# RWKV recurrence: output products of four chunks in one group, grams over 64 rows, wider zero products over the whole recurrence, and three more weight tiles for the experts

## The chip, the cores and the metric

One Trainium2 chip, one of its cores. The metric is the time of the program on the device in microseconds; lower is better. TensorE is called PE below, VectorE DVE, ScalarE ACT, GpSimd POOL, SyncE SP.

## The reference, cut to what matters

A backbone of two layers over 512 latent tokens and 256 context tokens of width 1024, all in float32. Layer 0 mixes attention with a convolution; layer 1 mixes RWKV-7 time mixing with a neighbourhood attention. Each layer ends in a mixture of 16 experts. The change lies in layer 1.

```python
def wkv7_step(S, inp):
    r, w, k, v, a, b = inp
    sa = jnp.einsum('bhvk,bhk->bhv', S, a)
    S = S * w[:, :, None, :] + sa[..., None] * b[:, :, None, :] + v[..., None] * k[:, :, None, :]
    return S, jnp.einsum('bhvk,bhk->bhv', S, r)
...
    y = head_group_norm(y_lat[0] + y_lat[1], gn_g, gn_b) * lat[6]
...
    gate, idx = lax.top_k(jnp.swapaxes(aff, 1, 2), cap)
    xs = jax.vmap(lambda hb, ib: hb[ib])(h, idx)
    hid = jax.nn.silu(jnp.einsum('becd,edf->becf', xs, w1)) * jnp.einsum('becd,edf->becf', xs, w3)
    ys = jnp.einsum('becf,efd->becd', hid, w2) * gate[..., None].astype(h.dtype)
```

The recurrence runs over the context and then the latent tokens, forwards and backwards, for 8 heads of 64 channels. Outputs of both directions are summed; only those of latent tokens are used, since layer 1 is the last.

## The kernel before, in words

The recurrence is computed in chunks of 64 tokens: 4 of context and 8 of latents. Two heads share the 128 partitions. Four pairs of heads times two directions are eight chains, n = 0 to 7; even n run forwards, odd n backwards, and n // 2 is the pair.

`rw_prep` (L1719 on) loads the decays, keys and queries of a chain, scales them and builds the grams G: 12 chunks x 2 heads of products `BK` by `RA` (L1763), four chunks to a group, each head to a PSUM bank of its own. `BK` holds zeros in the 64 rows that belong to the other head, and both operands are taken with all 128 rows. `rw_prep2` transposes `BK` (L1787). `rw_inverse` (L1922, L1930, L1945, L1959) inverts a triangular matrix for every chunk.

`rw_chain` (L1791 on) is the serial part, 12 steps a chain. A step multiplies the gram by the values (L1802) and the state by the queries (L1805), copies the sum out (X1, on ACT, L1807), multiplies it by the inverse (L1810), copies that into `UV` (L1812), and forms the next state `Z` from `pz` (L1817, then DVE L1821; POOL L1826 scales a copy). From step 4 on, the chunk is a latent one, and its output is accumulated in a bank `py`, which takes both directions of a pair of heads: per head a product `UV` by `G` (128 rows, 64 columns, L1836) and one `Z` by `RA` (64 rows, 64 columns, L1837). The bank is opened at step 4 of the forward chain by a product of zeros; at the end of the backward chain a term is added (L1842) and the sum copied to `yT`. There is one such bank.

`rw_run` advances everything in rounds n = -2 to 8 of 18 turns: in each turn the chain two or three times, the inverse of the chain two rounds ahead, the preparation of the one three rounds ahead, and the neighbourhood attention (`na_att`, L1426 to L1469). After each advance of the chain comes a zero product (`warm`, L1856): 128 rows and columns of zeros in bfloat16 by 224 columns, added to the open bank, as long as there is one. Rounds 6 and 7 also run `tail`: normalisation of finished heads and the output projection (`proj`, L545).

What is written is not the order that runs. A scheduler lays out each engine's queue ahead of time by its own model of the durations; a priority of 1000 is given to the chain. A queue is then executed in its fixed order.

The weights go through a ring of tiles of 1 MB, loaded by SP in a fixed sequence (`Ring.fill`, L150). A pool of tiles serves the phases that it is opened for. For the experts of layer 1 (phase 4) there are 9 tiles, opened at the end of the recurrence, and 8, opened in `layer1` when the projection's weights are done. The experts follow: `mix_tile` normalises, computes affinities and chooses tokens (`topk`, `choose`), `gather` fetches the rows of the first two experts (L684), and `experts` multiplies (w1 and w3 in L749, w2 in L815). Memory is cut from two arenas, "main" and "side". `open_x` reserves the residual X (4 x 1024 words) and `xT0` in one pool, which is held until the end of the experts.

Of the kernel before, what the change touches and what calls it, by code (L numbers as in the profile page):

```python
# [189 lines left out]
class Kern:  # L190
# [312 lines left out]
    def open_x(self, n=NT):  # L503

        self.right = ExitStack()
        xres = self.right.enter_context(self.arena.pool(1, True, ("m",)))
        self.X = [xres.tile([128, D], FT, name=f"X{t}") for t in range(n)]
        self.xT0 = xres.tile([128, 8, 128], FT, name="xT0")

    def open_ring(self, i):  # L510
        self.mring = ExitStack()
# [177 lines left out]
    def experts(self, i, ep, g2, cg2, with_ctx):  # L689
# [187 lines left out]
        if with_ctx:  # L877
            cT[0] = self.cT0
        more = ExitStack()
        with self.tc.manual_schedule(engines={mybir.EngineType.PE}):  # L880
            for p in range(8):
                H(p, 0)
                if p == i == 0:
                    more.enter_context(self.ring.open(self.arena, MOE_RING[1], (1,)))
                if p + 1 < 8:
                    prep_x(p + 1, 4)
                    prep_c(p + 1, 4)
                if p:
                    W2(p - 1, 1)
                H(p, 1)  # L890
                W2(p, 0)
            W2(7, 1)
# [342 lines left out]
    def layer1(self):  # L1235
        nc, tc, I = self.nc, self.tc, self.I
        with ExitStack() as ph:
# [36 lines left out]
            with ExitStack() as post:  # L1274
                self.rw_run(rw, post, yT, naT)
                self.open_ring(1)
                self.banks(NA_BANKS)
                for _ in self.rw_out(self.op, yT, 3):
                    pass
                todo = []  # L1280
                for t in range(4):
                    now = self.mix_tile(t, [yT, naT], (2, 3))
                    for f in now[:2]:
                        f()
                    if t == 3:

                        self.mix_done()
                        self.oring.close()
                        cs.close()
                        ph.enter_context(self.ring.open(self.arena, 8, (4,)))  # L1290
                    for f in todo:
                        f()
                    todo = now[2:]
                for f in todo:
                    f()
            self.moe(1, False)
        self.right.close()

# [296 lines left out]
    def rw_run(self, es, post, yT, naT):  # L1595
        nc, S, sets = self.nc, self.S, self.sets
        with ExitStack() as ae:
# [3 lines left out]
            py = {}  # L1601
            att = self.na_att(ap, naT)
            due = 0.0
            self.warmp = None
            emp = iter(())
            for n in range(-2, 9):
                chain = self.rw_chain(S[n], py, n // 2, yT[:, n // 2]) if 0 <= n < 8 else emp
# [11 lines left out]
                for i in range(18):  # L1619
                    if n >= 6 and i % 3 == 2:  # L1620
                        next(tail, None)
                    for x in range(2 + (i == 17)):
                        self.prio(chain, 1000)
                        self.warm(224)
                    self.prio(inv, 1000 if n < 0 else 0)
                    if i >= 3:
                        self.prio(prep2, 1000 if n < 0 else 0)
                    if i >= 6:
                        self.prio(prep, 1000 if n < 0 else 0)
                    due += ATT[min(n + 2, 3)][i]  # L1630
                    while due >= 1:
                        due -= 1
                        next(att, None)
# [81 lines left out]
    def rw_prep(self, hp, d, S):  # L1715
# [41 lines left out]
        for g in range(3):  # L1757
            ps = [self.bank("A") for h in range(2)]
            for a in range(4):
                c = 4 * g + a  # L1760
                i0 = c if g == 0 else IR(c)
                for h in range(2):
                    nc.tensor.matmul(ps[h][:, 128 * a:128 * a + 128], BK[:, c, 2 * h:2 * h + 2].rearrange("p a t -> p (a t)"),  # L1763
                                     RA[:, i0:i0 + 2].rearrange("p a t -> p (a t)"), start=True, stop=True)
            for h in range(2):
                p = ps[h]
                if g == 0:
# [24 lines left out]
    def rw_chain(self, S, pys, hp, y):  # L1792
# [1 line left out]
        nc, st = self.nc, self.st  # L1794
        d, RA, G, BKn, dec, UV, Q = (S[x] for x in ("d", "RA", "G", "BKn", "dec", "UV", "Q"))
        order = ORDER[d]
        Z = None
        p = self.bank(f"c{d}")
        px, pu, pz = p[:, 0:64], p[:, 64:128], p[:, 128:192]
        for i, c in enumerate(order):  # L1800
            for h in range(2):
                nc.tensor.matmul(px[HB[h]], G[HQ[h], h, IA(c)], UV[HQ[h], c, h], start=True, stop=(i == 0))  # L1802
            if i:
                for h in range(2):
                    nc.tensor.matmul(px[HB[h]], RA[HQ[h], IA(c)], Z[HQ[h]], start=False, stop=True)  # L1805
            X1 = st.tile([128, 64], FT, name=f"X1{d}")
            nc.scalar.activation(X1, px, AF.Copy)  # L1807
            yield
# [6 lines left out]
            if i < 11:  # L1815
                for h in range(2):
                    nc.tensor.matmul(pz[HQ[h]], BKn[:, c, h], UV[:, c, h], start=True, stop=True)  # L1817
                Zn = st.tile([128, 64], FT, name=f"Z{d}", bufs=4)
                de = dec[:, order[i + 1]:order[i + 1] + 1]
                if i:  # L1820
                    nc.vector.scalar_tensor_tensor(Zn, pz, de, Zd, op0=OP.mult, op1=OP.add)  # L1821
# [3 lines left out]
                    Zd = st.tile([128, 64], FT, name=f"Zd{d}", bufs=1)  # L1825
                    nc.gpsimd.tensor_scalar(Zd, Zn, dec[:, order[i + 2]:order[i + 2] + 1], None, op0=OP.mult)  # L1826
            if i >= 4:
                if i == 4 and d == 0:
                    pys[hp] = self.bank("y")
                    nc.tensor.matmul(pys[hp], self.zero[:, 0:128], self.zero, start=True, stop=False)  # L1830
                    self.warmp = pys[hp]
                py = pys[hp]
                for h in range(2):
                    q = HQ[h]
                    o = py[q, 64 * (c - 4):64 * (c - 4) + 64]
                    nc.tensor.matmul(o, UV[:, c, h], G[:, h, IR(c)], start=False, stop=False)  # L1836
                    nc.tensor.matmul(o, Z[q], RA[q, IR(c)], start=False, stop=False)  # L1837
            Z = Zn
            yield
        if d == 1:  # L1840
            self.warmp = None
            nc.tensor.matmul(py, self.ident, y, start=False, stop=True)  # L1842
            nc.scalar.activation(y, py, AF.Copy)

    def prio(self, g, o):

# [257 lines left out]
```

## Time and profile before

| | us |
|---|---|
| median of 3 runs | 2452.12 |
| lowest and highest | 2444.69, 2467.73 |
| the profiled execution | 2454.27 |
| its span, first to last instruction | 2452.5 |
| recurrence of layer 1, in the profile | 1417 to 1890 |
| experts of layer 1, from their first full stretch of loads | 1967 to 2452.5 |

A busy share is the time in which an engine has an instruction in hand. PE's instructions overlap, so a row's duration is longer than the distance to the next start. A float32 product is recorded as two instructions (two passes), except a transpose; a bfloat16 one as one. In the rows, 64*64 is the part of the array that is used (rows by columns), 64x64 the shape of what is written.

### The profile page before, as it was taken

What the parts mean: (1) busy time and instruction counts of PE and PEld (TensorE: products, weight loads), DVE (VectorE), ACT (ScalarE), POOL (GpSimd) and SP (SyncE); (2) the same over time, 40 slices, a digit from 0 to 9 for tenths busy, and PEclk for the clock granted to TensorE, in tenths of its full rate; (3) what the DMA queues carried; (4) which work ended last, traced back from release to release, by engine and by line L of the source; (5) the groups of instructions that cost most, each with busy time, mean ns of one, the idle gap of its engine ahead of it and who ended that gap; (6) DMA issues with size and microseconds to landing.
All of it is one profiled execution on the core that took longest, in us unless ns stands there. A gap on an engine that the chain in (4) does not pass through costs nothing.

```text
span 2452.5 us, 36218 instructions
## 1 busy us (share of the span) xinstructions
PE 2193.5 (89%) x14792; PEld 1166.6 (48%) x14792; DVE 962.6 (39%) x2135; ACT 602.7 (25%) x1658; POOL 487.6 (20%) x477
## 2 busy tenths in 40 slices
PE   5999799997999999995999989999999598877786
PEld 2774455553333333333778757777664432222222
DVE  3896556663111111114225678776432610000000
ACT  3113544421111101103333334444430110000000
POOL 3434300100001111005644332332111000000000
PEclk8999899998999999998999998999899699999999
DMA  9546301146999999993234362321333399999996
GB/s 393 230 147 231 133 18 44 44 175 245 377 394 395 392 405 405 377 368 96 83 112 147 106 197 52 77 77 49 113 131 122 152 394 414 413 414 414 414 414 248
DMA packets 161813, 577.08 MB, mean 235 GB/s; under 512 B 72544, under 2 KB 84704, under 8 KB 102896
## 3 DMA queue, kind: packets, MB, share of 16 engines
q1 hardware_dynamic: 119024, 503.64, 52.0%
q10 hardware_dynamic: 34816, 42.30, 5.0%
q0 software_dynamic: 7808, 28.84, 4.5%
q8 instruction: 116, 1.90, 0.3%
q14 instruction: 49, 0.40, 0.0%
HBM read 535.90 MB, written 38.83 MB: 234 GB/s over the span
## 4 chain that ended last, share of the span: by engine, by line
PE 27%; DMA 18%; DVE 4%; issue 2%; POOL 1%; ACT 1%; POOLq 0%; SPq 0%; ACTq 0%; DVEq 0%
DMA side<-moe_w 9%; DMA main<-moe_w 8%; PE b L1369 3%; PE b L1521 3%; PE b L1763 2%; PE b L749 2%; PE b L545 2%; PE b L1837 1%; PE b L815 1%; PE b L1836 1%; PE b L1856 1%; PE b L1523 1%; PE b L1426 1%; PE b L1446 1%; PE b L1817 1%
## 5 line engine op out<-in xcount | busy, mean ns | idle before, releaser
L749 PE MATMUL b<-main 128*64 128x512 f32 x888 | 253.9, 600 | 0.0
L815 PE MATMUL b<-main,side 128*64 128x512 f32 x744 | 236.9, 605 | 17.4 <-DMA main<-moe_w 16.6
L749 PE MATMUL b<-main,side 128*64 128x512 f32 x688 | 216.9, 611 | 14.6 <-DMA main<-moe_w 14.6
L1344 POOL TENSOR_TENSOR wlo<-main,whi 128x1024 fp32r<-128x1024 f32 x43 | 128.2, 2987 | 150.3 <-ACT whi L1343 146.2
L815 PE MATMUL b<-side 128*64 128x512 f32 x280 | 123.5, 611 | 24.5 <-DMA side<-moe_w 24.5
L749 PEld LDWEIGHTS b<-main 128*64 128x64 f32 x888 | 77.5, 138 | 130.3 <-issue 128.0
L775 DVE SCALAR_TENSOR_TENSOR side<-side,b 128x512 f32<-128x512 f32 x32 | 22.0, 687 | 284.5 <-ACT side L774 284.5
L1026 DVE SCALAR_TENSOR_TENSOR main<-main 128x783 f32<-128x783 f32 x120 | 130.0, 1139 | 0.9
L815 PEld LDWEIGHTS b<-main,side 128*64 128x64 f32 x744 | 68.9, 139 | 126.3 <-issue 95.2
L749 PE MATMUL b<-side 128*64 128x512 f32 x208 | 98.8, 623 | 22.4 <-DMA side<-moe_w 22.4
L666 PE MATMUL b<-main,side 128*32 128x512 f32 x792 | 116.6, 602 | 0.0
L749 PE MATMUL b<-side,main 128*64 128x512 f32 x264 | 115.5, 594 | 0.0
L790 DVE SCALAR_TENSOR_TENSOR side<-side,b 64x512 f32<-64x512 f32 x16 | 10.9, 679 | 264.1 <-ACT side L789 264.1
L783 ACT ACTIVATE side<-b 128x512 f32<-128x512 f32 x32 | 19.1, 597 | 366.5 <-PE b L782 366.5
L749 PEld LDWEIGHTS b<-main,side 128*64 128x64 f32 x688 | 63.7, 139 | 95.3 <-issue 65.9
L666 PE MATMUL b<-side 128*32 128x512 f32 x232 | 103.1, 594 | 0.9 <-DMA side<-moe_w 0.9
L874 POOL DMA_INDIRECT c_keep<-main x16 | 21.3, 1331 | 366.1 <-DVE main L862 356.5
L545 PE MATMUL b<-main,side 128*128 128x512 f32 x192 | 86.4, 597 | 0.5 <-DVE side L1231 0.5
L1343 ACT ACTIVATE whi<-main 128x1024 fp32r<-128x1024 f32 (+1 forms) x45 | 46.9, 1047 | 158.5 <-PE b L972 38.6
L774 ACT ACTIVATE side<-b 128x512 f32<-128x512 f32 x32 | 19.1, 597 | 254.8 <-PE b L749 254.8
L815 PEld LDWEIGHTS b<-side 128*64 128x64 f32 x280 | 34.5, 139 | 72.1 <-DMA side<-moe_w 36.8
L1826 POOL TENSOR_SCALAR side<-side,main 128x64 f32<-128x64 f32 x60 | 34.7, 579 | 169.1 <-DVE side L1821 126.5
(451 smaller groups left out, 4574.2 us busy)
## 6 DMA issues: line engine op xcount, KB each, us to landing
main<-moe_w SPq DMA_DIRECT2D x290, 1024.0 KB, 13.4
side<-moe_w SPq DMA_DIRECT2D x94, 1024.0 KB, 17.4
main<-ada_w SPq DMA_DIRECT2D x48, 1024.0 KB, 8.1
rw_lkb<-main ACTq DMA_DIRECT2D x24, 384.0 KB, 2.8
main<-od_w_rw SPq DMA_DIRECT2D x7, 1024.0 KB, 5.5
main<-od_w_in SPq DMA_DIRECT2D x6, 1024.0 KB
main<-rw_lkb SPq DMA_DIRECT2D x32, 192.0 KB, 3.6
main<-ev_w_conv SPq DMA_DIRECT2D x4, 1024.0 KB, 13.8
```

What stands on the lines that cost most here:

```text
L545: nc.tensor.matmul(p, l[:, t * 128:(t + 1) * 128], w[k], start=(k == ks[0]), stop=(k == ks[-1]))
L666: self.nc.tensor.matmul(hc[32 * u:32 * u + 32], cT[:, k, c0:c0 + 32], W[we][:, kk], start=(k == 0), stop=(k == 7), tile_position=(0, 32 * u))
L749: nc.tensor.matmul(h[64 * e:64 * e + 64], xT[p][:, k, 64 * e:64 * e + 64], W[w, e][:, kk], start=(k == 0), stop=(k == 7))
L815: nc.tensor.matmul(y[d][64 * e:64 * e + 64], hidT[p, j][:, a, 64 * e:64 * e + 64], W[e][:, kk, 512 * d:512 * d + 512], **fl)
L1026: nc.vector.scalar_tensor_tensor(cv[:, c], convT[:, c, k:k + W], dw[:, c, k:k + 1], cv[:, c], op0=OP.mult, op1=OP.add)
L1343: nc.scalar.activation(hi, w, AF.Copy)
L1344: (e or nc.gpsimd).tensor_tensor(lo, w, hi.bitcast(FT), op=OP.subtract)
L1369: nc.tensor.matmul(pb[t], a[:, k, c], b[:, kk], start=(k == m == 0), stop=(k == 7 and m == 2))
L1426: nc.tensor.matmul(p1[:, :n], q, kv[:, b0 * 128:b0 * 128 + n], start=True, stop=True)
L1521: nc.tensor.matmul(px.rearrange("p (r j c) -> p r j c", r=8, j=4), a[:, k], r8(b, k), **fl)
L1763: nc.tensor.matmul(ps[h][:, 128 * a:128 * a + 128], BK[:, c, 2 * h:2 * h + 2].rearrange("p a t -> p (a t)"), RA[:, i0:i0 + 2].rearrange("p ...
L1826: nc.gpsimd.tensor_scalar(Zd, Zn, dec[:, order[i + 2]:order[i + 2] + 1], None, op0=OP.mult)
```

## The change

Five edits. The outputs of chunks are no longer issued at every step from 4 on: they are collected, and issued at steps 7 and 11 for four chunks at once, first all `UV` by `G`, then all `Z` by `RA`; ten instead of four states are kept. The grams take only the 64 rows of their head. The zero products are 320 columns wide. The output bank is opened earlier: for the first pair of heads ahead of the rounds, for the others at step 1 of the forward chain, and zero products run as soon as it is open. X gets a pool of its own, which is released ahead of the experts; three more ring tiles are opened at the start of the experts of layer 1.

```diff
@@ open_x
-        xres = self.right.enter_context(self.arena.pool(1, True, ("m",)))
+        self.xright = self.right.enter_context(ExitStack())
+        xres = self.xright.enter_context(self.arena.pool(1, True, ("m",)))
         self.X = [xres.tile([128, D], FT, name=f"X{t}") for t in range(n)]
-        self.xT0 = xres.tile([128, 8, 128], FT, name="xT0")
+        self.xT0 = self.right.enter_context(self.arena.pool(1, True, ("m",))).tile([128, 8, 128], FT, name="xT0")
@@ experts
         more = ExitStack()
+        if i:
+            more.enter_context(self.ring.open(self.arena, 3, (4,)))
@@ layer1
                 for f in todo:
                     f()
+            self.xright.close()
             self.moe(1, False)
@@ rw_run
-            self.warmp = None
+            self.open_sums(py, 0)
...
-                        self.warm(224)
+                        self.warm(320)
@@ rw_prep
                 for h in range(2):
-                    nc.tensor.matmul(ps[h][:, 128 * a:128 * a + 128], BK[:, c, 2 * h:2 * h + 2].rearrange("p a t -> p (a t)"),
-                                     RA[:, i0:i0 + 2].rearrange("p a t -> p (a t)"), start=True, stop=True)
+                    nc.tensor.matmul(ps[h][:, 128 * a:128 * a + 128], BK[HQ[h], c, 2 * h:2 * h + 2].rearrange("p a t -> p (a t)"),
+                                     RA[HQ[h], i0:i0 + 2].rearrange("p a t -> p (a t)"), start=True, stop=True)
@@ rw_chain
+            if i == 1 and hp not in pys:
+                self.open_sums(pys, hp)
...
-                Zn = st.tile([128, 64], FT, name=f"Z{d}", bufs=4)
+                Zn = st.tile([128, 64], FT, name=f"Z{d}", bufs=10)
...
             if i >= 4:
-                if i == 4 and d == 0:
-                    pys[hp] = self.bank("y")
-                    nc.tensor.matmul(pys[hp], self.zero[:, 0:128], self.zero, start=True, stop=False)
-                    self.warmp = pys[hp]
                 py = pys[hp]
-                for h in range(2):
-                    q = HQ[h]
-                    o = py[q, 64 * (c - 4):64 * (c - 4) + 64]
-                    nc.tensor.matmul(o, UV[:, c, h], G[:, h, IR(c)], start=False, stop=False)
-                    nc.tensor.matmul(o, Z[q], RA[q, IR(c)], start=False, stop=False)
+                outs.append((c, Z))
+                if i in (7, 11):
+                    for c, z in outs:
+                        for h in range(2):
+                            nc.tensor.matmul(py[HQ[h], 64 * (c - 4):64 * (c - 4) + 64], UV[:, c, h], G[:, h, IR(c)], start=False, stop=False)
+                    for c, z in outs:
+                        for h in range(2):
+                            q = HQ[h]
+                            nc.tensor.matmul(py[q, 64 * (c - 4):64 * (c - 4) + 64], z[q], RA[q, IR(c)], start=False, stop=False)
+                    outs = []
...
+    def open_sums(self, pys, hp):
+        pys[hp] = self.bank("y")
+        self.nc.tensor.matmul(pys[hp], self.zero[:, 0:128], self.zero, start=True, stop=False)
+        self.warmp = pys[hp]
```

In the changed kernel the lines of the chain move: L1806 and L1809 are the former L1802 and L1805, L1816 is L1810, L1823 is L1817, L1767 is L1763, L1870 is L1856; L1840 and L1844 are the output products.

On PE in the first chain, at one of its output steps, the queue of before holds the two kinds of output products in turn, with the state's product between the heads and a zero product behind:

```order
L1810 MATMUL b_9139<-side,main 64x64 x2
L1693 MATMUL b_8302<-main 128x256
L1693 MATMUL b_8305<-main 128x512
L1836 MATMUL b_9297<-main 64x64
L1837 MATMUL b_9297<-main,side 64x64
L1817 MATMUL b_9139<-main 64x64 x2
L1836 MATMUL b_9297<-main 64x64
L1837 MATMUL b_9297<-main,side 64x64
L1856 LDWEIGHTS main
L1856 MATMUL b_9297<-main 128x224
```

and the changed queue, at the fourth chunk of a group (b_8369 is the output bank, b_9765 and b_10338 the banks of the two chains that run):

```order
L1816 MATMUL b_9765<-side,main 64x64 x2
L1823 MATMUL b_10338<-side 64x64 x2
L1944 MATMUL b_10096<-main 32x16 x7
L1450 MATMUL b_8765<-main,side 128x128 x3
L1944 MATMUL b_10096<-main 32x16 x8
L1767 MATMUL b_10254<-main 128x128
L1840 MATMUL b_8369<-side,main 64x64
L1823 MATMUL b_9765<-main 64x64 x2
L1840 MATMUL b_8369<-side,main 64x64
L1844 MATMUL b_8369<-side 64x64 x8
L1806 MATMUL b_10338<-side,main 64x64 x2
L1809 MATMUL b_10338<-side,main 64x64 x2
```

The second kind now stands in a run of eight; the first kind has been pulled forward, one head on either side of L1823.

On PE at the first step of the first chain, the queue of before goes from the last projection product (L1521) through the chain (L1802, L1810):

```order
L1521 MATMUL b_8336<-Thi,wlo 128x512
L1802 MATMUL b_9139<-main 64x64 x2
L1693 MATMUL b_7901<-main 128x256
L1693 MATMUL b_7904<-main 128x512
L1810 MATMUL b_9139<-side,main 64x64 x2
```

and the changed one has the bank opened (L1856) and zero products (L1870) there, two of them ahead of the chain's first product (L1806):

```order
L1525 MATMUL b_8336<-Thi,wlo 128x512
L1856 LDWEIGHTS main
L1856 MATMUL b_8369<-main 128x512
L1870 LDWEIGHTS main
L1870 MATMUL b_8369<-main 128x320
L1870 LDWEIGHTS main
L1870 MATMUL b_8369<-main 128x320
L1806 MATMUL b_9215<-main 64x64 x2
```

Up to the fifth L1816 there are 97 of them.

On SP, the loads for the experts from the output projection's weights on, before:

```order
L150 DMA side<-od_w_out 128x2048 x4
L150 DMA main<-moe_w 128x2048 x3
L150 DMA side<-moe_w 128x2048 x2
L150 DMA main<-moe_w 128x2048 x6
L150 DMA side<-moe_w 128x2048 x2
L150 DMA main<-moe_w 128x2048 x10
```

and in the changed kernel:

```order
L150 DMA side<-od_w_out 128x2048 x3
L150 DMA main<-moe_w 128x2048 x3
L150 DMA side<-moe_w 128x2048 x2
L150 DMA main<-moe_w 128x2048 x5
L150 DMA side<-moe_w 128x2048 x2
L150 DMA main<-moe_w 128x2048
L150 DMA side<-moe_w 128x2048 x3
L150 DMA main<-moe_w 128x2048 x9
```

The three loads into "side" behind the seventeenth are the new tiles; they lie where the buffers of the choice of tokens lay.

## Rows read from the trace of the kernel before

**Rows 1.** Busy time of the engines by stage: start:end, length, then for each engine busy us and instructions, the granted clock of TensorE, the share of the DMA engines, GB/s.

```profile
0.00:1417.00 1417.00, 1300.09 (x7453) 694.70 (x7453) 589.07 (x1208) 372.53 (x944) 330.82 (x278) 0.96 0.61 230
1417.00:1890.00 473.00, 450.11 (x5529) 313.36 (x5529) 282.34 (x693) 186.88 (x617) 120.95 (x169) 0.92 0.33 100
1890.00:1967.00 77.00, 47.12 (x177) 30.47 (x178) 46.25 (x158) 13.86 (x37) 8.34 (x9) 0.65 0.44 166
1967.00:2452.50 485.50, 396.15 (x1640) 128.06 (x1636) 44.97 (x78) 29.44 (x60) 27.50 (x21) 0.96 0.97 393
```

**Rows 2.** Waits of PE between 1417 and 1890 us: who waited for whom, us in total, times, the longest. The first three of nine entries, which sum to 16.8 us.

```profile
PE b L1810 <- ACT side L1807: 3.0, 9, 0.5
PE b L1426 <- DMA side<-na_qkv: 3.0, 1, 3.0
PE b L1802 <- DVE side L1821: 2.3, 3, 1.5
```

**Rows 3.** Time line of PE's products at 1611 to 1615.5 us: start, us until the last one ended, line, tiles, part of the array, shape, count.

```profile
1611.74 1.16 PE L1763 MATMUL b<-side,main 128*128 128x128 f32 x8
1612.73 0.45 PE L1856 MATMUL b<-main 128*128 128x224 bf16 x3
1613.12 0.33 PE L1836 MATMUL b<-main,side 128*64 128x64 f32 x2
1613.37 0.33 PE L1837 MATMUL b<-main,side 64*64 64x64 f32 x2
1613.63 0.33 PE L1836 MATMUL b<-main,side 128*64 128x64 f32 x2
1613.89 0.32 PE L1837 MATMUL b<-main,side 64*64 64x64 f32 x2
1614.14 0.46 PE L1856 MATMUL b<-main 128*128 128x224 bf16 x3
1614.44 0.49 PE L1446 MATMUL b<-main,side 128*128 128x128 f32 x3
1614.86 0.33 PE L1802 MATMUL b<-side,main 64*64 64x64 f32 x4
1615.03 0.28 PE L1805 MATMUL b<-side,main 64*64 64x64 f32 x4
1615.14 0.28 PE L1802 MATMUL b<-main 64*64 64x64 f32 x4
1615.26 0.28 PE L1805 MATMUL b<-side,main 64*64 64x64 f32 x4
1615.47 0.33 PE L1446 MATMUL b<-main,side 128*128 128x128 f32 x1
```

**Rows 4.** Waits of PE from 1967 us to the end, columns as in rows 2.

```profile
PE b L815 <- DMA side<-moe_w: 24.5, 13, 5.9
PE b L749 <- DMA side<-moe_w: 22.4, 14, 3.8
PE b L815 <- DMA main<-moe_w: 16.6, 11, 3.4
PE b L749 <- DMA main<-moe_w: 14.6, 12, 2.3
```

**Rows 5.** A stretch in the middle of the experts, columns as in rows 1.

```profile
2200.00:2300.00 100.00, 79.31 (x322) 25.52 (x320) 9.86 (x18) 6.57 (x14) 6.61 (x5) 0.97 1.02 412
```

**Rows 6.** Busy time in single stretches, columns as in rows 1.

```profile
1420.00:1450.00 30.00, 24.60 (x183) 18.53 (x182) 19.53 (x35) 10.89 (x28) 11.89 (x15) 0.83 0.66 209
1470.00:1500.00 30.00, 28.55 (x389) 22.42 (x389) 22.43 (x48) 9.38 (x26) 6.84 (x9) 0.66 0.16 45
1500.00:1730.00 230.00, 222.48 (x3456) 167.08 (x3449) 166.99 (x431) 113.70 (x377) 72.74 (x101) 0.98 0.26 66
1730.00:1770.00 40.00, 36.55 (x475) 25.11 (x473) 18.24 (x53) 14.44 (x54) 6.63 (x13) 0.70 0.38 135
...
1934.00:1967.00 33.00, 8.20 (x32) 3.95 (x33) 21.67 (x100) 1.87 (x6) 3.02 (x3) 0.54 0.19 61
```

**Rows 7.** Groups of PE's instructions between 1417 and 1890 us: line, tiles, shapes, count, busy us, mean ns of one, idle time before and what ended it.

```profile
L1763 PE MATMUL b<-main 128*128 128x128 f32 x240 | 42.5, 322 | 1.7 <-DVE main L1768 1.5 <-DVE main L1751 0.2
L1856 PE MATMUL b<-main 128*128 128x224 bf16 x236 | 37.5, 268 | 0.0
...
L1763 PE MATMUL b<-side,main 128*128 128x128 f32 x96 | 17.1, 325 | 0.9 <-POOL main L1751 0.6 <-DVE side L1768 0.2
```

**Rows 8.** Time line of PE's products, columns as in rows 3: a run of transposes at 1734 us with the instruction behind it, and a run of zero products at 1816 us.

```profile
1734.68 0.47 PE L1787 MATMUL b<-main 64*128 64x64 f32 x8
1735.08 0.33 PE L1802 MATMUL b<-main 64*64 64x64 f32 x4
...
1816.43 1.71 PE L1856 MATMUL b<-main 128*128 128x224 bf16 x16
1818.07 0.33 PE L1836 MATMUL b<-main 128*64 128x64 f32 x2
```

**Rows 9.** Time line between the recurrence and the experts: SP's loads (start, us until the last one was issued), PE's last products of the choice and first ones of the experts, and the gather on POOL.

```profile
1913.31 67.61 SPq L150 DMA_DIRECT2D main<-moe_w  x10
...
1952.67 0.42 PE L622 MATMUL b<-main,side 16*128 16x16 f32 x2 [0.80 <-DVE side L614]
1960.15 1.97 PE L406 MATMUL b<-main,side 128*128 128x128 f32 x8 [7.07 <-DMA side<-x_scr,main]
1962.05 4.35 PE L749 MATMUL b<-main 128*64 128x512 f32 x14
...
1955.61 1.12 POOL L684 DMA_INDIRECT side<-x_scr,main  x1 [33.41 <-DVE main L639]
```

More of the change, by code (lines that the diff above doesn't have):

```diff
@@ L1796, in rw_chain @@
         order = ORDER[d]
-        Z = None
+        Z, outs = None, []
         p = self.bank(f"c{d}")
```

## The prediction

> **What bounds the kernel now.** I read the busy time by stage first [rows 1]. The recurrence of the RWKV layer stands from 1417 to 1890 us: TensorE (PE) is busy for 450 of 473 us there, VectorE for 282, the DMA engines for a third, and the clock is 0.92. Next the waits of PE in that stretch: the entries add up to 16.8 us, the longest 3.0 us [rows 2]. So PE's own queue sets the length of this stage, and what an instruction costs is the distance from its start to the next start, not its recorded duration, which overlaps the next one. The time line of PE shows these distances [rows 3]. Then the stage behind: experts of layer 1, from 1967 to the end. There PE waits for weights for 24.5+22.4+16.6+14.6 = 78 us [rows 4], and the DMA engines move 412 GB/s at a share of 1.02 [rows 5]: it is bound by the transfers. Between them, 1934 to 1967, the transfers almost stop (share 0.19, [rows 6]).
>
> **The outputs.** Each of 64 chunk steps issues four products in the order L1836, L1837, L1836, L1837. They start at 1613.12, .37, .63, .89, and the next instruction at 1614.14: 1.02 us a step, a quarter of a microsecond for each small product [rows 3]. A float32 product is two records, so "x2" is one. Where the products of the two heads stand side by side and the shape of array tile stays, as in L1802 and L1805, eight products take 1614.86 to 1615.47 = 0.61 us [rows 3]: the two heads start within a few ns of each other, and a change of shape is paid once. 64 x 1.02 = 65 us is what the stage pays now at full clock; I take 62, since some of these products stand beside L1817, whose shape (128 rows by 64 columns) is L1836's.
> Afterwards the order shows the first kind (L1840) not in eights but mostly in singles on both sides of L1823, in the shape of L1823, so with no change of shape but with the heads unpaired; the second kind (L1844) stands in 16 runs of eight. Runs of eight: 16 x 0.61 = 10 us. The 128 singles: 0.61/8 = 0.08 us if they paired, 0.25 us if each paid a change of shape; inside a run two paired products take 0.12 us (1615.14 to 1615.26), and one product alone in its shape needs its two passes one after the other just the same, so 0.12 each: 15 us (10 to 32). Sum 25 us, a gain of 37 us (20 to 42).
>
> **The grams.** L1763 multiplies 128 rows of which 64 are zero. Eight records, that is four products, take 1611.74 to 1612.73 = 0.99 us, so 0.25 us a product [rows 3]; 168 of the 192 products lie in this stage (336 records, [rows 7]): 41 us. With 64 rows each, the two heads use different halves of the array. The nearest row is the transposes of L1787: same 64 by 128 shape, half as many columns; eight take 1734.68 to 1735.08 = 0.40 us [rows 8], in pairs. A pair of grams would cost what one costs now, which halves 38 us of pure streaming to 19. Not all pair: the order has 26 of 52 runs of odd length, so 97 pairs instead of 84: 22 us, gain 16. Against this stands the change of shape. A gram beside a zero product or an attention product has that product's shape now (1612.73 follows without a jump), and will not afterwards.
> The Trainium skill says so outright: "Changing tiling mode (not just tile) drains the TensorE" (TensorEngine Tiling (Array Packing), Key Properties). The trace agrees: 0.25 us for an output product alone against 0.08 in a run [rows 3]. By that rule the gram's gain is 16 less the switches below; without it 16.
> 31 sides of the 52 runs stand beside a full-array product, at about 0.1 us for the jump (0.39 us for three zero products ahead of L1836, against 3 x 0.096): 3 us. Gain 13 us (-3 to 19).
>
> **The zero products.** Now 236 [rows 7] of 224 columns. Sixteen take 1816.43 to 1818.07 = 1.64 us [rows 8], three 0.39 [rows 3]; the difference, 13 for 1.25 us, gives 0.096 each. 320 columns: 0.137. The loop will issue 37 for each of the two rounds ahead of the chains, 37 in round 0, 34 in rounds 2, 4, 6 and 36 in the odd ones: 74 + 37 + 102 + 144 = 357. 357 x 0.137 - 236 x 0.096 = 49 - 23 = 26 us more on PE. What hides them is idle PE: the order puts 97 of them ahead of the fifth step of the first chain, where PE is busy for 24.6 of 30 us today (1420 to 1450, [rows 6]). I count 6 us as filling that gap and 20 as added. If the gap stayed open for other reasons it is 26; if the clock gains from it, less.
>
> **The clock.** Stretches below full clock: 1420 to 1450 at 0.83, 1470 to 1500 at 0.66, 1730 to 1770 at 0.70 [rows 6]. In work lost: 30 x 0.17 + 30 x 0.34 + 40 x 0.30 = 27 us. Each follows gaps of PE. Zero products from the first step on should keep the first of them, 5 us; the other two I leave, since PE's order is fixed and a zero product queued behind a waiting product cannot run early. Bounds: 0 to 27 us gained, and as much lost if the shorter queue waits more often.
>
> **New waits.** With some 30 us less on PE, the attention loads, the preparation on VectorE and the steps of the chains come late more often. 17 us of PE waits stand there today [rows 2]; I add a third, 6 us (0 to 15). The output groups themselves delay nobody: their sum is read only when the second direction ends. Opening the bank at step 1 instead of step 4 waits for the copy that closes the previous pair, as before; outputs are later, so nothing is tighter. L1823, which feeds the next state, now stands behind one single instead of two products and a change of shape.
>
> **Three weight tiles.** The DMA queue's last load ahead of the experts waits: its ten loads from 1913.31 spread over 67.6 us [rows 9], until products release tiles after 1962.05. Three more tiles are 3 x 1.049 MB / 412 GB/s = 7.6 us of transfers that move into the gap. They use memory that the choice of tokens holds: two can start when the last choice product has read it (1952.67), the third when the gathered rows are transposed (1960.15 and 2 us) [rows 9]. All three stand in front of loads that could not start before 1966. The gather issued at 1955.61 now shares the engines with two of them; I take 1 us off. Gain 6.5 us (3 to 7.6). The experts' own buffers move to the released rows of X, which are free by then.
>
> **Sum.** In the recurrence -37 - 13 + 20 - 5 + 6 = -29 us; experts -6.5. Together -35.5. The profiled execution took 2454.27 us (span 2452.5 and 1.8 around it), 2 us above the median of 2452.12. 2454.3 - 35.5 = 2419.
>
> **Rivals.**
> First, the clock comes back as well: the denser queue holds full clock through the two late stretches, 22 us more: 2397. For it: they are the only long stretches at half clock between 1470 and 1890. Against it: the one at 1730 starts at a late attention load, which zero products don't shorten.
> Second, the gain is spent in waits: PE stops being what ends last, and the preparation (VectorE 167 of 230 us between 1500 and 1730, [rows 6]) and the loads set the pace. Then perhaps a third of the 29 us arrives: 2454.3 - 10 - 6.5 = 2438. For it: the order was laid out by a scheduler that may have assumed other durations, and bunches of 12 to 24 zero products stand where it expects PE idle. Against: 17 us of waits in 473.
> Third, the other side: the heads' halves do not overlap. It decides if two neighbouring small products start a full pass apart. Then a run of eight costs 8 x 0.12 = 1 us (16 us), the singles at a full pair of passes with their jump 0.25 (32 us): outputs -14; grams nothing back and 31 new jumps, +3; zero products +26, all on the path; the waits +6 us as above. -14 + 3 + 26 + 6 = +21; with the weights at -3: 2472. Against it: L1802, L1805 and L1787 overlap in the trace in just these shapes.
> Fourth, the weights bring nothing, because the three loads delay the gather by what they save: 2425.
>
> **How the numbers follow.** Forecast (2405 to 2432) 0.53; first rival (below 2405) 0.18; second (2432 to 2448) 0.18; third 0.05, of which half ends slower by over 1%; fourth 0.06. A measurement of this kernel can tell about 1% from no change: faster by over 1% means below 2427.6. That holds for the first rival, 0.41 of the forecast's 0.53 and 0.05 of the fourth: 0.64. Slower (above 2476.6): 0.03. The same: 0.33. The range leaves out 1 in 10 on each side: 2394 to 2446.
>
> **What would show it.** Right: the output products in 16 runs of eight at about 0.6 us; grams in pairs that start a few ns apart, 0.11 us per pair of records; the recurrence near 444 us; share of transfers between choice and experts up by three loads, and the experts' stage about 6 us shorter measured from the first expert product. Wrong: pairs that start 50 ns or more apart; PE waits of 30 us and more in the stage; the clock below 0.9 there; the gather landing later by several us.

## The result and the profile after

The changed kernel takes 2474.8 us (median; 2456.95 to 2497.37) against 2451.8: a ratio of 1.008, 95% interval 1.006 to 1.010. The ratio leaves out the two slowest of the changed kernel's 20 executions, which lay over 1.5% above its fastest; by the medians it is 1.009. It is slower, by a little less than the 1% that the prediction counted as a change, where 2419 us and a range of 2394 to 2446 were forecast.

The busy time by stage after the change answers to [rows 1]; the stages are cut as there, some 6 us behind the last product of the chains and 5 us behind the first of the experts.

```profile
1417.00:1925.00 508.00, 475.07 (x5648) 323.98 (x5644) 286.76 (x695) 186.95 (x617) 112.64 (x168) 0.84 0.31 95
1925.00:2001.00 76.00, 45.90 (x176) 29.99 (x178) 44.65 (x156) 13.93 (x37) 8.33 (x9) 0.64 0.51 192
2001.00:2475.70 474.70, 397.89 (x1640) 131.86 (x1636) 44.62 (x78) 29.43 (x60) 27.48 (x21) 0.98 0.98 396
```

The recurrence is 35 us longer (508 against 473) and the experts 10.8 shorter (474.7 against 485.5). In the recurrence the number of PE's instructions barely moved; the clock fell from 0.92 to 0.84. Work lost to the clock, length times (1 - clock), is 508 x 0.16 = 81 us against 473 x 0.08 = 38: 43 us more. The recurrence grew by 35, so the other edits together gave back 8. The stretches of [rows 6], and two more:

```profile
1420.00:1450.00 30.00, 30.00 (x230) 21.07 (x229) 18.13 (x31) 9.84 (x23) 11.21 (x12) 1.00 0.65 202
1470.00:1500.00 30.00, 28.97 (x314) 22.38 (x314) 22.42 (x55) 9.16 (x25) 8.59 (x10) 0.50 0.21 55
1500.00:1730.00 230.00, 214.36 (x2869) 154.76 (x2869) 144.54 (x364) 95.08 (x318) 51.98 (x82) 0.79 0.21 51
1730.00:1770.00 40.00, 35.87 (x560) 24.88 (x559) 24.48 (x57) 18.69 (x65) 12.86 (x19) 0.87 0.38 98
...
1480.00:1510.00 30.00, 30.00 (x421) 23.91 (x422) 17.67 (x48) 9.46 (x25) 5.51 (x8) 0.50 0.13 28
1680.00:1720.00 40.00, 40.00 (x412) 30.18 (x411) 22.53 (x61) 11.61 (x38) 5.29 (x8) 0.50 0.01 2
```

The first stretch did come to full clock, and the quiet middle (0.98 before) lost it. In the last two rows PE has no gap at all and runs at half clock, 1.2 GHz: PE is not waiting there. PE's time line at a run of grams (1433) and a run of outputs (1552), both at full clock, and at another run of grams at half clock (1684):

```profile
1433.04 1.16 PE L1767 MATMUL b<-side,main 64*128 64x128 f32 x8
1434.13 0.33 PE L1806 MATMUL b<-main 64*64 64x64 f32 x4
...
1552.71 0.68 PE L1844 MATMUL b<-main,side 64*64 64x64 f32 x16
1553.32 0.34 PE L1823 MATMUL b<-main 128*64 128x64 f32 x4
...
1684.07 1.97 PE L1470 MATMUL b<-side 128*64 128x128 f32 x14
1685.97 2.07 PE L1767 MATMUL b<-main 64*128 64x128 f32 x8
1687.97 0.48 PE L1806 MATMUL b<-main 64*64 64x64 f32 x4
```

Sixteen records of L1844, a run of eight products, take 0.61 us, as forecast; all 16 runs are there, and at half clock one takes 1.05 (at 1502.28). Eight records of grams take 1.09 us at full clock and 2.00 us at half, against 0.99 in [rows 3]. These eight start one after the other, so by their spacing they belong to one head: the scheduler had laid the two heads' grams apart. At 1.09 they gain nothing on before, where a run of eight also takes 1.09 between products of other shapes (at 1512.61, for one).

### The profile page after: what moved, and what is told of

The parts are those of the page before. It is cut to its first block, busy times and chain, and to the rows that moved or that the text cites. A ratio compares the mean times of both kernels' runs of the same rounds, so it can differ in the third digit from the quotient of the medians.

```text
span 2475.7 us, 36461 instructions
## 1 busy us (share of the span) xinstructions
PE 2218.0 (90%) x14913; PEld 1178.6 (48%) x14913; DVE 966.3 (39%) x2135; ACT 603.2 (24%) x1658; POOL 481.4 (19%) x477
## 5 line engine op out<-in xcount | busy, mean ns | idle before, releaser
L750 PE MATMUL b<-main 128*64 128x512 f32 x1480 | 430.8, 604 | 24.0 <-DMA main<-moe_w 24.0
L750 PEld LDWEIGHTS b<-main 128*64 128x64 f32 x1480 | 130.5, 138 | 252.7 <-issue 199.7
L750 PE MATMUL b<-side,main 128*64 128x512 f32 x568 | 221.3, 596 | 8.0 <-DMA side<-moe_w 8.0
L816 PE MATMUL b<-main 128*64 128x512 f32 x320 | 100.7, 609 | 27.0 <-DMA main<-moe_w 25.6
L816 PE MATMUL b<-main,side 128*64 128x512 f32 x376 | 112.2, 594 | 0.0
L750 PEld LDWEIGHTS b<-side,main 128*64 128x64 f32 x568 | 65.4, 136 | 77.1 <-issue 60.6
L934 DVE TENSOR_SCALAR main<-b,main 128x128 f32<-128x128 f32 x120 | 40.9, 403 | 116.9 <-PE b L724 94.2
L775 ACT ACTIVATE side<-b 128x512 f32<-128x512 f32 x32 | 19.1, 597 | 247.0 <-PE b L750 247.0
L816 PE MATMUL b<-side,main 128*64 128x512 f32 x192 | 69.6, 597 | 7.3 <-DMA side<-moe_w 5.1
L932 ACT ACTIVATE main<-b,main 128x128 f32<-128x128 f32 x120 | 45.1, 456 | 119.0 <-PE b L406 60.9
L816 PEld LDWEIGHTS b<-main 128*64 128x64 f32 x320 | 28.9, 139 | 89.4 <-DMA main<-moe_w 44.2
L875 POOL DMA_INDIRECT out<-main x16 | 22.6, 1415 | 238.4 <-DVE main L869 191.8
```

The lines of the kernel that those rows point to most:

```text
L750: nc.tensor.matmul(h[64 * e:64 * e + 64], xT[p][:, k, 64 * e:64 * e + 64], W[w, e][:, kk], start=(k == 0), stop=(k == 7))
L816: nc.tensor.matmul(y[d][64 * e:64 * e + 64], hidT[p, j][:, a, 64 * e:64 * e + 64], W[e][:, kk, 512 * d:512 * d + 512], **fl)
L875: nc.gpsimd.indirect_dma_start(out=self.acc(i, s), out_offset=at, in_=v[n * e:n * e + n], in_offset=None, compute_op=OP.add)
L932: nc.scalar.activation(out[:, a], pt[:, a], AF.Identity, bias=sh[:, k, s:s + 1], scale=gs[:, k, s:s + 1])
L934: nc.vector.tensor_scalar(out[:, a], pt[:, a], gs[:, k, s:s + 1], sh[:, k, s:s + 1], op0=OP.mult, op1=OP.add)
```

## Experiments

Ratios are to the kernel before, with 95% intervals. First, what lowered the clock.

**Grams of 128 rows in the changed kernel** (e2):

```diff
-BK[HQ[h], c, ...], RA[HQ[h], i0:i0 + 2]
+BK[:, c, ...],     RA[:, i0:i0 + 2]
```

> The changed kernel with its grams of 128 rows as before, the rest as changed. Theory A (the zero products ran ahead and left the clock alone, grams of 64 rows are innocent): the same low clock between 1460 and 1510 and 1680 and 1720, and 0 to 15 us slower than the changed kernel, 2475 to 2490. Theory B (products on half of the array's rows count for less, and so the clock fell): the granted clock of the recurrence comes back to 0.92 and the kernel takes about 2474 - 46 + 13 = 2441 us.

Measured 0.992 (0.989 to 0.995). The clock of the recurrence is 0.92 again (row below). B's 2441 us stands against 2439.2 measured. What A held to be the cause, the bunched zero products, is still in this kernel.

**Grams of 64 rows alone in the kernel before** (e5): the reverse edit.

> The kernel before with nothing but the grams of 64 rows. Theory A (the zero products alone explain the clock): they are spread as before here, so the clock of the recurrence stays at 0.92 and the grams bring 3 to 19 us, 2435 to 2450 against 2453. Theory B (a product on half of the rows counts for less, so the clock falls): the granted clock in the recurrence falls to 0.80 to 0.87 and the kernel is 15 to 40 us slower than before, 2468 to 2493.

Measured 1.022 (1.018 to 1.026), 2516 us, past B's range, with a clock of 0.79. A falls. But the scheduler also orders 64-row grams differently, so rows and order were still mixed.

**The rows alone, order kept** (e16). The order is laid out for grams of 128 rows, then each gram is replaced:

```diff
+for h, m in GRAMS:   # after scheduling; operands start at row 64 * h
+    half[m.name] = replace(m, ins=ap, tile_size=(64, 128), tile_position=(64 * h, 0))
+b.instructions = [half.pop(m.name, m) for m in b.instructions]
```

> The kernel before with its grams turned to 64 rows after the order was laid out: every engine runs the same instructions in the same order with the same waits as before, and only the 384 records read 64 rows in place of 128. Theory B (rows): the clock of the recurrence falls below 0.88 and the kernel is 20 to 50 us slower than before, 2475 to 2505. Theory D (the order that the scheduler gives to 64-row grams): the clock stays at 0.92 and the kernel gains what the paired grams save, 5 to 15 us, 2440 to 2448. The version with 64 rows and its own order took 1.022 of before.

Measured 1.026 (1.021 to 1.030): with the same instructions in the same order, the rows that are read cost 63 us by themselves, more than B's range. The stretch of [rows 1] and the instructions of [rows 3] in this run:

```profile
1417.00:1890.00 473.00, 455.77 (x5178) 323.46 (x5178) 264.32 (x658) 181.83 (x592) 108.88 (x159) 0.73 0.28 81
```

```profile
1676.55 0.71 PE L1763 MATMUL b<-side,main 64*128 64x128 f32 x8
1677.20 0.46 PE L1856 MATMUL b<-main 128*128 128x224 bf16 x3
1677.59 0.33 PE L1836 MATMUL b<-main,side 128*64 128x64 f32 x2
1677.85 0.33 PE L1837 MATMUL b<-main,side 64*64 64x64 f32 x2
```

Where the clock is full and the heads stand side by side, the eight records take 0.65 us instead of 0.99. If all 336 stood so, this would give 336 / 8 x 0.34 = 14 us, the size that was forecast. In this run only 46 pairs of records out of 168 start together, so an estimate from these rows is 46 / 4 x 0.34 = 4 us; the others follow each other, since the order of before keeps most grams of one head together too. The clock, at 0.73, takes many times that. The Trainium skill (TensorEngine Tiling (Array Packing), Theoretical Speedup) gives up to two times for a small dimension of 64 or less; here it is 1.5 times for the run of eight, and a loss for the kernel.

**The same on the fastest version** (e17, based on e8 below).

> The same on the fastest version so far (outputs of four chunks, three tiles, early bank, zero products of 224 columns): its order is kept, its grams read 64 rows. Theory B: 30 us or more above that version, so 0.994 of before or more, with the clock below 0.88. Theory D: 0.975 to 0.982 of before.

Measured 0.996 (0.994 to 0.999) against 0.982: 1.4% or 35 us more, as B has it. The recurrences of e2, e5, e16, e17 and e8, in this order, one row of each:

```profile
1417.00:1883.00 466.00, 439.10 (x5631) 305.83 (x5629) 281.79 (x691) 187.16 (x614) 113.83 (x165) 0.92 0.34 102
```

```profile
1417.00:1950.00 533.00, 514.65 (x5535) 350.46 (x5534) 289.52 (x692) 190.22 (x619) 118.24 (x169) 0.79 0.29 89
```

```profile
1417.00:1971.00 554.00, 533.83 (x5541) 364.12 (x5540) 285.00 (x695) 189.16 (x620) 117.21 (x169) 0.75 0.28 85
```

```profile
1417.00:1894.00 477.00, 448.01 (x5655) 313.33 (x5653) 288.86 (x695) 188.06 (x619) 120.37 (x169) 0.85 0.33 101
```

```profile
1417.00:1865.00 448.00, 419.88 (x5618) 301.45 (x5618) 284.63 (x690) 185.51 (x614) 114.56 (x162) 0.92 0.35 106
```

Of these five, the two with 128 rows have 0.92 and the three with 64 rows 0.85 or less.

**Products by themselves, without gaps** (e7).

> The kernel before with five blocks of products on zeros put ahead of the recurrence, on fp32 tiles and without gaps: 200 of 128 rows by 128 columns, 200 pairs of 64-row products on the two halves of the rows, 200 of 128 rows, 200 of 64 rows all on the first half, 200 of 128 rows. Theory B: the clock is 1.0 in the blocks of 128 rows and falls to 0.5 in the block on one half, and in the block of pairs it stays at 1.0 if the two run side by side. Theory A: 1.0 in all five. By the rows of before, a product of 128 columns starts every 105 ns at full clock, a pair takes the time of one, and the blocks add 5 x 21 = 105 us.

```profile
1418.00:1474.00 56.00, 56.00 (x456) 52.30 (x456) 20.38 (x30) 9.20 (x18) 6.54 (x8) 1.00 0.55 177
1474.00:1518.00 44.00, 44.00 (x790) 44.00 (x792) 0.00 (x0) 0.00 (x0) 0.00 (x0) 1.00 0.01 2
1519.00:1563.00 44.00, 44.00 (x396) 44.00 (x396) 0.00 (x0) 0.00 (x0) 0.00 (x0) 1.00 0.01 1
1564.00:1608.00 44.00, 44.00 (x396) 44.00 (x396) 0.00 (x0) 0.00 (x0) 0.00 (x0) 1.00 0.00 1
1609.00:1653.00 44.00, 44.00 (x396) 44.00 (x395) 0.00 (x0) 0.00 (x0) 0.00 (x0) 1.00 0.00 1
```

One row a block, the first shared with other work. 1.0 in all five, the fourth (one half alone) included: B was wrong here. In the second block the pairs do run side by side, 790 records in the time of 396. I had also counted a product's two records as one, at 111 ns and not 105 each, so a block takes 45 us and not 21. Half the rows alone do not lower the clock in a dense run. This probe and the next ran once each.

**Products diluted by changes of shape** (e11).

```diff
+for rows in (0, 128, 0, 64, 0, 128, 0, 64, 0):      # 0: a gapless block of 200
+    for j in range(100):
+        matmul(pa, zero[0:rows, 0:128], zero[0:rows])            # bf16, 512 columns
+        matmul(pb[0:32, 0:16], z32[0:32, 0:32], z32[0:32, 32:48])  # fp32
```

> The kernel before with blocks of products on zeros ahead of the recurrence. A gapless block of 200 products of 128 rows stands first and between the others; the others are 100 times a bf16 product of 512 columns and a fp32 product of 32 rows and 16 columns, which changes the shape twice, once with 128 rows in the large product, then with 64, both twice over. Theory B (rows count): the clock stays at 1.0 in the blocks with 128 rows, at some 0.42 us a round, and falls to 0.5 in those with 64, at some 0.8 us a round. Theory C (only the order that the scheduler gave to the 64-row grams matters, or the time in which the array streams): the two kinds of block read alike, either both at 1.0 or both at 0.5.

```profile
1476.00:1523.00 47.00, 45.74 (x290) 22.28 (x294) 0.00 (x0) 0.00 (x0) 0.00 (x0) 1.00 0.00 1
1524.00:1568.00 44.00, 44.00 (x397) 44.00 (x395) 0.00 (x0) 0.00 (x0) 0.00 (x0) 1.00 0.00 1
1569.00:1640.00 71.00, 71.00 (x295) 26.73 (x294) 0.00 (x0) 0.00 (x0) 0.00 (x0) 0.52 0.00 0
1641.00:1687.00 46.00, 46.00 (x400) 46.00 (x400) 0.00 (x0) 0.00 (x0) 0.00 (x0) 0.97 0.00 1
1688.00:1735.00 47.00, 45.74 (x289) 22.20 (x292) 0.00 (x0) 0.00 (x0) 0.00 (x0) 1.00 0.00 1
...
1781.00:1852.00 71.00, 71.00 (x294) 26.63 (x294) 0.00 (x0) 0.00 (x0) 0.00 (x0) 0.52 0.00 0
```

```profile
1500.31 0.39 PE L1613 MATMUL b<-main 128*128 128x512 bf16 x1
1500.63 0.23 PE L1614 MATMUL b<-main 32*32 32x16 f32 x2
1500.79 0.39 PE L1613 MATMUL b<-main 128*128 128x512 bf16 x1
...
1599.56 0.60 PE L1613 MATMUL b<-main 64*128 64x512 bf16 x1
1600.10 0.28 PE L1614 MATMUL b<-main 32*32 32x16 f32 x2
1600.31 0.60 PE L1613 MATMUL b<-main 64*128 64x512 bf16 x1
```

The rounds differ only in the rows of the large product: full clock and 0.48 us a round with 128, half clock and about 0.72 us (71 us for 98 rounds) with 64, twice. C falls. The recurrence is such a mixture of short products and changes of shape. There the 64-row grams also add changes of shape, since they no longer have the shape of the zero and attention products beside them, and e16 does not separate these from the rows; here, where the number of changes is the same, the rows alone do it.

**Wider zero products as a remedy** (e15): `self.warm(512)` for 320 in the changed kernel.

> The changed kernel, its grams of 64 rows included, with zero products of 512 columns in place of 320. They take 355 x 0.080 = 28 us more by TensorE's time at full clock (0.136 us for 320 columns). Theory B (the 64-row grams lowered the clock because half of the rows counts for less): the wider products put the rows back, the clock of the recurrence rises from 0.84 to 0.92, worth some 40 us, and the kernel takes 2475 + 28 - 40 = 2463, 1.00 to 1.005 of before. Rival (the order in which the grams stand lowered it): the clock stays at 0.84 and the kernel takes 2503, 1.02.

Measured 1.013 (1.008 to 1.019), 2497 us, with the clock at 0.84 as without. Both halves of B's expectation fail, and the rival's come nearer: the clock as it said, the time 6 us short of its 2503. That the order alone lowered the clock is nevertheless out, by e16, which kept the order. The zero products are not where the clock is low: the changed kernel issues one in 1680 to 1720, and e15 none in 1480 to 1510 (one row of each, zero products alone):

```profile
1680.00:1720.00 40.00, 0.47 (x1) 0.15 (x1) 0.50 0.01 2
...
1480.00:1510.00 30.00, 0.00 (x0) 0.00 (x0) 0.50 0.08 18
```

**Undoing early opening or grouping, with 64-row grams kept.** e3 opens the bank at step 4 of each pair; e4 issues the outputs at every step.

> The changed kernel with the bank of the sums opened at step 4 as before, so that the first four steps of each pair have no zero products. Theory A (zero products that no step of the chain holds back run ahead in a bunch): about half of them are still free to run between steps 4 and 7 and 7 and 11, so the clock comes back in part, 2455 to 2465. Theory B (64-row grams): no better, 2475 or more. A third, that the sheer count of early zero products takes time on TensorE at full clock: some 100 x 0.136 = 13 us less, 2461, with the clock as low as in the changed kernel.

> The changed kernel with the four output products of a head pair issued at every step from 4 on, as before; the bank is still opened early, the grams are of 64 rows and the zero products of 320 columns. Theory A: the zero products behind step 4 are held back by the outputs again and spread, the clock of the recurrence returns to 0.92 or more, which gives some 40 us, and the 16 us or more that grouping saved are lost: 2440 to 2458. Theory B (64-row grams): the clock stays at 0.83 to 0.85 and the kernel is slower than the changed one, 2490 to 2510.

e3: 1.004 (1.001 to 1.007), clock 0.81; e4: 1.011 (1.007 to 1.015), clock 0.87. e3, at 2468 us, lies between A's time and B's and comes nearest to the third account (2461, with the clock as low); e4, at 2487, is next to B's. Neither brings the clock back to 0.92, so neither edit is the cause by itself.

Second, what the other edits are worth without the 64-row grams.

**Tiles alone** (e1).

> The kernel before with nothing but the three tiles more in the ring of the last experts' part, and the pool of X split for them. All theories of the recurrence: 3 to 7.6 us less than before (2444 to 2449 against 2452), all of it after the choice of the experts, with the recurrence as before to 2 us. Rival: the experts' part gives nothing, 2452, because the wait moves to the last tiles.

Measured 0.994 (0.992 to 0.997): 14 us (8 to 21). In its profile the first expert product starts at 1971.2 and the span ends at 2451.8, 480.6 us later, against 490.4 in before (1962.05 in [rows 9] to 2452.5). That is 9.8 us, above the forecast's 7.6. The mechanism is the forecast's: the 77 us ahead of this stage moved 207 GB/s x 77 us = 15.9 MB, against 12.8 in before [rows 1], three loads more.

```profile
1899.00:1976.00 77.00, 43.90 (x170) 29.39 (x170) 44.74 (x155) 13.44 (x37) 8.34 (x9) 0.65 0.54 207
1976.00:2451.80 475.80, 395.12 (x1645) 131.16 (x1640) 44.64 (x78) 29.43 (x60) 27.48 (x21) 0.99 0.97 394
```

That the recurrence stays as before to 2 us is not shown: it was 9 us longer in this execution (row below), which took 2453.5 us, 11 more than e1's median.

**Outputs and tiles** (e9), **the same with the bank opened early** (e8), **with 320 columns at the late opening** (e13).

> The kernel before with the outputs of four chunks together and the three tiles, with grams of 128 rows, zero products of 224 columns and the bank opened at step 4. If the clock of the recurrence stays near 0.92, the outputs give their 35 us and the tiles 10: 2408. If the zero products, which no output step holds back any more, run ahead and leave the clock at 0.85 or less, some 30 us of that go: 2438, no better than the changed kernel with grams of 128 rows.

> The changed kernel with grams of 128 rows and zero products of 224 columns; the bank is still opened early. Against the version with outputs and tiles alone (0.988 of before) it tells what the 121 zero products more cost: at 0.1 us each 12 us, 0.993; if they keep the clock up at the start of the recurrence they pay for themselves, 0.986 to 0.990. Against the one with 320 columns too (0.992): 357 x 0.04 = 14 us less if the columns cost their time, 0.986.

> The kernel before with the outputs of four chunks together, the three tiles and zero products of 320 columns, with the bank opened at step 4: the changed kernel without its 64-row grams and its early opening. Against outputs and tiles alone (0.988): 236 x 0.04 = 9 us more if the columns only cost their time, 0.992; if they hold the clock up, 0.982 to 0.988. The same kernel with 64-row grams took 1.004 of before, so by theory B some 30 us less than that, 0.990.

e9: 0.988 (0.984 to 0.991), 2429 us, with a clock of 0.91 but more waits. The recurrences of e1 and of e9, a row each: PE is idle for 482 - 457 = 25 us and for 451 - 410 = 41.

```profile
1417.00:1899.00 482.00, 457.12 (x5535) 317.09 (x5534) 286.65 (x695) 188.12 (x619) 118.98 (x169) 0.92 0.32 98
```

```profile
1417.00:1868.00 451.00, 409.67 (x5508) 292.78 (x5507) 287.47 (x691) 183.52 (x614) 113.81 (x164) 0.91 0.36 106
```

e8: 0.982 (0.980 to 0.984), 2415 us, the fastest median of all and faster than both kernels; the early zero products pay for themselves. e13: 0.988 (0.986 to 0.991), no different from e9 by its interval. e3 is e13 with grams of 64 rows: 1.004 against 0.988 is 38 us more, a fifth comparison that goes B's way, with e2, e5, e16 and e17.

**Other groupings.** e10 keeps the outputs at every step but issues both heads' product with UV, then both with Z; e12 puts two chunks together; e14 is e8 with two chunks.

> The kernel before with the three tiles and, at every step from 4 on, the same four output products in another order: the product with UV for both heads, then the one with Z for both. The shape changes twice in a step and not four times, and the zero products stay tied to the steps. If a change of shape costs 0.1 us: 64 x 2 x 0.1 = 13 us from the recurrence and 10 from the tiles, 2430, with the clock as before. Rival: nothing from the order, because the scheduler places other products between them, 2443.

> The kernel before with the three tiles and the outputs of two chunks together, at steps 5, 7, 9 and 11, the rest as before. Two shape changes for two chunks in place of eight, and the zero products are held back by outputs twice as often as with four chunks. If what four chunks lack is the spread of the zero products, 0.980 to 0.985 of before; if the shape changes alone count, between the two that are measured, 0.988.

> The changed kernel with grams of 128 rows, zero products of 224 columns and the outputs of two chunks together: the version that took 0.982 of before, with outputs at steps 5, 7, 9 and 11. If holding the zero products back more often helps as much as two chunks against four did in the profiles with the late opening (441 us of recurrence against 447), 0.980; rival: no difference or a little more for the shape changes, 0.982 to 0.986.

0.988 (0.984 to 0.991), 0.987 (0.985 to 0.990), 0.983 (0.978 to 0.987): e10, a reordering of four lines, is not told apart from e9; its time is as expected, its clock is not: 0.88 and not 0.92. So grams of 64 rows are not all that moves the clock: with 128 rows it lay between 0.88 (e10) and 0.94 (e14), with 64 between 0.75 (e16) and 0.87 (e4). Two or four chunks make no difference that these runs can tell.

## Why the prediction was wrong

**What bounds the kernel.** Right: PE's queue. What it missed is that its speed depends on what is in it.

**The outputs.** Nearly right on PE, too large for the stage. From each start to the next, the output records take 63 us in the trace of before, as forecast, and 31 in e9, where 25 was forecast. By the run times 0.9876 / 0.9942 = 0.993 is left of it (e9 against e1), 16 us against 37. The difference stands in PE's idle time, 41 us in e9 against 23 in before: the second rival's mechanism. The profiles of e1 and e9 differ by 31 us in the recurrence, but the one execution was 11 us above its median and the other 7 below, so that figure is too large.

**The grams.** The step that failed: "Gain 13 us (-3 to 19)". It priced the columns and the jumps at full clock and put the clock's answer to half the rows at nothing. By e2 and the changed kernel (1.008 / 0.9918 = 1.016) the edit costs 40 us, alone 54 (e5), with the order kept 63 (e16). The pairing itself failed as well: the 97 were 71 pairs of products and 26 singles, so 142 pairs of records, and 44 pairs of records start together in the stage; runs of one head stand in the trace instead (1433.04). From each start to the next, the 336 records take 58 us after and 55 before, not 41: [rows 3] shows one of the shorter runs, and some of the others ran at half clock.

**The clock.** "-5 us" with "0 to 27 us gained, and as much lost if the shorter queue waits more often": 43 us were lost, with PE idle for only 10 us more. "Each follows gaps of PE" was read as the cause; the changed kernel shows half clock without gaps. The first stretch, 5 us, was right. So was the sign that was named for being wrong, "the clock below 0.9 there".

**The zero products.** +20 forecast; early opening and 320 columns together cost 0.9918 / 0.9876 = 1.004, 10 us (e2 against e9), which is not clear of the noise. Opening early alone gains 13 us (e8 against e9), and 320 columns on top cost 24 (e2 against e8). At the late opening the same columns cost nothing that can be told (e13 against e9), so it is the width together with the early opening that costs.

**New waits.** +6 forecast; PE's idle time rose from 23 to 33 us, the nearest to right. The 17 us that it started from are the first nine waits alone; the others of that list bring them to 22.

**Three tiles.** -6.5 forecast (3 to 7.6), 14 measured (8 to 21), and 9.8 between the profiles from the first expert product on: the right mechanism, sized too small. In the changed kernel PE's waits for weights, 78 us in [rows 4], are shorter each, 1.8 us at the longest in the groups of L816 (L815 before) against 5.9:

```profile
PE b L816 <- DMA main<-moe_w: 25.6, 20, 1.8
PE b L750 <- DMA main<-moe_w: 24.0, 19, 2.8
PE b L750 <- DMA side<-moe_w: 8.0, 6, 1.5
PE b L816 <- DMA side<-moe_w: 5.1, 5, 1.7
```

They sum to 62.7, 15 us less than before. That is more than three loads' 7.6 us of transfers; why was not tried.

**Sum of what was measured.** -14 (tiles) - 16 (outputs) + 10 (zero products) + 40 (grams) = +20 us, 0.008 x 2452. Each was measured on top of the one before it (e1, e9, e2, the changed kernel), so they add up by construction and the sum is no check; in another order the shares differ, as the grams' 35 to 63 us show. None of the four rivals had this cause: the third came nearest in time (2472) by luck, by heads that don't overlap, and where they stand side by side they do (e7, e16).

**Still open.** How rows, columns and changes of shape weigh together in the recurrence; why the order of e10 lowered the clock; and why the scheduler separates the heads.

## What to carry to other kernels

Before you cut the rows of a product that was padded with zeros, look at the granted clock: in a queue of short products and shape changes the padding may be what holds it, and a saving forecast at 13 us can cost 35 to 63. Price a filler by where the order puts it, not by its count: here 40 us at half clock held a single zero product, and wider ones elsewhere gave nothing back. To test such an edit, keep the order and change the one operand, since a scheduler changes the order along with it.

## What was not expected of the hardware

TensorE at half clock with no gap: 71 of 71 us busy at 0.52 in the diluted block of 64 rows, beside 45.74 of 47 at 1.00 with 128. The Trainium skill (TensorE: Matmul & The Clock Gate, What's actually happening) sets the clock by how busy PE has been recently; here the block that the profile shows as busier had the lower clock, though part of its busy share is the half clock itself, at which each product takes longer. A dense block of 64 rows on one half kept 1.00.
